# Two feed-forward layers: the activation of 14 column blocks turned by the DMA engines as two 16-bit planes, where TensorE had turned it

## The chip, the core and the metric

The kernel runs on one core of a Trainium2 chip, in float32 from end to end. The metric is the device time of one execution in microseconds (us), taken as the median of several runs. A profile is one further execution, recorded by the hardware profiler.

## What is computed

The reference is a decoder layer: a SwiGLU feed-forward layer, a mixing layer (retention and windowed attention), and a second SwiGLU layer, each on a normalised and modulated input. The change concerns the two feed-forward layers alone:

```
def swiglu(h, w_gu, w_down):
    gate, up = jnp.split(h @ w_gu, 2, axis=-1)
    return (jax.nn.silu(gate) * up) @ w_down
# S = 256 rows, D_MODEL = 2048, D_FF = 5632; called once on w_ffn1_* and once on w_ffn2_*
```

## The kernel before

A float32 product is made from halves. Each weight tile `raw` is split into a rounded part `wh` (cast on ACT, line 334) and a remainder `wl` (subtraction on DVE, line 335). The activation is held split in the same way, as `hh` and `hl` for the input of a feed-forward layer, and as pair tiles `a` for the input of the down product. Each 128x512 product then takes three matmuls: line 326 (high times high), line 327 (low times high) and line 328 (high times low).

`gemm` (lines 383 to 388) makes 512 output columns for both halves of 128 rows. It walks over K in blocks of 512 (`kb`). Each block is one DMA of 1 MB on the SP queue (`load`, line 311, four `raw` buffers) and two **half steps**. A half step is one cast, one subtraction and 12 matmuls. `wh` and `wl` have three buffers each (`wsp`), so ACT and DVE work up to three half steps ahead of TensorE.

`ffn_up` (lines 545 to 550) goes over blocks of 512 of the 5632 columns. For each it runs one gemm for the gate and one for the up half, 16 half steps in all. Then `swiglu_up` works on two tiles of 128x512, one for each half of the rows: Silu on ACT (line 537), the multiplication on DVE (line 538), and `transpose_to` (lines 412 to 417), which turns the tile on TensorE in four 128x128 pieces into a PSUM bank (line 416) and copies that to the tile `slot` that the down product reads (line 417). The first layer's blocks 0 to 5 are made in another loop at the start of the program. `ffn_up` makes blocks 6 to 10 of the first layer, and blocks 0 to 10 of the second, whose first gate half is already there when it begins.

`step()` (lines 299 to 307) is called after each K block of a gemm and advances a list of side work, `side`, by one. In the feed-forward layers this list is empty. `tick()` paces another stream beside the gemms: rows of `w_ada`, loaded on the SP queue and reduced on DVE (`ada_pass`, line 203).

Where an instruction stands on its engine is decided by the scheduler of the framework, for all engines but SP. `nc.any` leaves the choice of the engine to it as well. Each engine then runs its own list in order, and waits where it stands.

Of the kernel before, what the change touches and what calls it, by code (L numbers as in the profile page):

```python
# [8 lines left out]

F32 = mybir.dt.float32  # L10
F32R = mybir.dt.float32r
AF = mybir.ActivationFunctionType
ALU = mybir.AluOpType
AX = mybir.AxisListType
# [2 lines left out]
P = 128  # L17
S = 256
D = 2048
DFF = 5632  # L20
# [3 lines left out]
CH = 512  # L24
KB = 4
# [51 lines left out]
def layer_kernel(  # L77
# [22 lines left out]
    nc = tc.nc  # L100
# [15 lines left out]
    def nm(s):  # L116
        uid[0] += 1
        return f"{s}_{uid[0]}"
# [4 lines left out]
    def bank():  # L123
        return psm.tile([P, CH], F32, tag="ps", name=nm("ps"))

    def side_bank():
        return psd.tile([P, CH], F32, tag="pd", name=nm("pd"))

    def t512():
        return tmp.tile([P, CH], F32, tag="t512", name=nm("t"))  # L130
# [4 lines left out]
    def slot():  # L135
        return slots.tile([P, KD * S], F32, tag="slot", name=nm("slot"))

    def small(n, tag):
        return two.tile([P, n], F32, tag=tag, name=nm(tag))
# [27 lines left out]
    for j in range(D // CH):  # L167
        pt = acc_bank()
        nc.tensor.matmul(pt, ones, c_row[:, j * CH : (j + 1) * CH], start=True, stop=True)
        nc.scalar.activation(cact[:, j * CH : (j + 1) * CH], pt, AF.Silu)  # L170
    gains = one.tile([P, 3, KD], F32, tag="gains", name="gains")
# [125 lines left out]
    side = []  # L297
# [32 lines left out]
    def split(pool, tag, src, n, hi_engine="act"):  # L330
        k = src.shape[1]
        hi = pool.tile([P, 2, n], F32R, tag=tag + "h", name=nm(tag + "h"))[:, :k, :]
        lo = pool.tile([P, 2, n], F32R, tag=tag + "l", name=nm(tag + "l"))[:, :k, :]
        nc.scalar.copy(hi, src)  # L334
# [3 lines left out]
    def pair_tile():  # L338
        return asp.tile([P, 2, CH], F32, tag="a", name=nm("a"))

    class Held:


        def __init__(self):
            self.hi = one.tile([P, KD, S], F32R, tag="hh", name=nm("hh"))
            self.lo = one.tile([P, KD, S], F32R, tag="hl", name=nm("hl"))

# [3 lines left out]
    class Whole:  # L351
# [5 lines left out]
        def pair(self, k2, home=None):  # L357
# [3 lines left out]
            if home is None:  # L361
                home = pair_tile()
            hi, lo = (
                home[:, i].rearrange("p (k s) -> p k s", k=2).bitcast(F32R) for i in range(2)
            )
# [17 lines left out]
    def gemm(act, w, col0s, KT=KD):  # L383
        banks = [[acc_bank() for _ in range(NT)] for _ in col0s]
        for kb in range(KT // KB):
            gemm_part(act, w, col0s, banks, kb, KT)
            step()
        return banks

    def home_tile():  # L390

        return slots.tile([P, 2, KD * P], F32R, tag="slot", name=nm("home"))

# [18 lines left out]
    def transpose_to(dest, src_of, n, ps=None):  # L412

        ps = ps or bank()
        for j in range(n):
            nc.tensor.transpose(ps[:, j * P : (j + 1) * P], src_of(j), ident)  # L416
        nc.any.tensor_copy(dest, ps[:, : n * P])  # L417


    def rsqrt(v, n):  # L420

        r = small(n, f"rs{n}")
        q = small(n, f"rq{n}")
        nc.scalar.activation(r, v, AF.Sqrt)
        nc.vector.reciprocal(r, r)
        nc.vector.tensor_mul(q, r, r)
        nc.vector.tensor_mul(q, q, v)
        nc.vector.tensor_scalar(
            out=q, in0=q, scalar1=-0.5, scalar2=1.5, op0=ALU.mult, op1=ALU.add
        )  # L430
        nc.vector.tensor_mul(r, r, q)
        return r

    def square_sum(dest, src):
        nc.scalar.activation(side_bank(), src, AF.Square, accum_out=dest)  # L435

    def root_table():

        nc.scalar.activation(small(1, "root"), eps, AF.Sqrt)

    def inv_rms(ssq, t):
# [7 lines left out]
        )  # L449
        nc.scalar.activation(r, s, AF.Sqrt, bias=eps, scale=1.0 / D)  # L450
        nc.vector.tensor_scalar(
# [12 lines left out]
    def modulated(held, k, src, m_shift, act=False):  # L464
# [4 lines left out]
        if act:  # L469
            nc.scalar.activation(h, src, AF.Identity, bias=shift, scale=scale)  # L470
        else:
# [50 lines left out]
        square_sum(ssq[:, t * 4 + ci : t * 4 + ci + 1], xs)  # L522


    def swiglu_up(banks_g, banks_u, tiles, ci, parts=None):

        k0 = ci * KB
        dest = tiles[k0 // KD].rearrange("p (k s) -> p k s", s=S)
        kk = k0 % KD
        for t in range(NT):  # L530
            s = t512()
            g, u = banks_g[t], banks_u[t]
            if parts is not None:
                nc.vector.tensor_add(s, g, parts[0][t])
                nc.vector.tensor_add(parts[1][t], u, parts[1][t])
                g, u = s, parts[1][t]
            nc.scalar.activation(s, g, AF.Silu)
            nc.vector.tensor_mul(s, s, u)
            transpose_to(
                dest[:, kk : kk + KB, t * P : (t + 1) * P],  # L540
                lambda j: s[:, j * P : (j + 1) * P],
                KB,
            )

    def ffn_up(held, w, tiles, first, bg=None):
        for ci in range(first, DFF // CH):
            bg = bg or gemm(held, w, [ci * CH])[0]
            bu = gemm(held, w, [DFF + ci * CH])[0]
            swiglu_up(bg, bu, tiles, ci)
            bg = None  # L550

    ORDERED = {mybir.EngineType.PE, mybir.EngineType.DVE, mybir.EngineType.Activation}
# [144 lines left out]
    tiles = [slot(), part[0]]  # L697
# [102 lines left out]
    for g, ks in enumerate(groups):  # L800
        final = g == len(groups) - 1
        order = chunks if g % 2 == 0 else chunks[::-1]
        coming = iter(()) if final else group(groups[g + 1])
        due = 0 if final else 2 * len(groups[g + 1])
        stay = () if final else order[-2:]
        for i, n in enumerate(order):
            visit(n, ks, load_blocks(n, ks), n not in stay)
            last = len(order) - 2
            for _ in range((i + 1) * due // last - i * due // last if i < last else i == last):
                next(coming, None)  # L810
            if n in stay:
                continue
            if not final:
                to_parts(n)
            elif n % 2:
                swiglu_up(
                    banks.pop(n - 1), banks.pop(n), tiles, n // 2, (part_of(n - 1), part_of(n))
                )
    gate = gate_row()
    tiles.append(slot())  # L820
    place = two_rows()
    set_pace([(2, None, 0.5), (4, 1, None), (3, None, None)], 154, place, AQ)
    ffn_up(held, gu, tiles, EARLY)
    gate_load(gate, 2)
    wi = w_in[0]
# [240 lines left out]
    def gates(p):  # L1066

        sg = slot().rearrange("p (g i t n) -> p g i t n", g=2, i=2, t=NT)
        for g, off in ((0, O_GR), (1, O_GS)):
            for i in range(2):  # L1070
                b = in_chunk(off + (2 * p + i) * CH)
                for t in range(NT):
                    nc.scalar.activation(sg[:, g, i, t, :], b[t], AF.Sigmoid)
        return sg

    first = gates(0)
# [44 lines left out]
    tiles = [slot() for _ in range(3)]  # L1121
    set_pace([(8, None, 0.5)], 160, raw_row, 2)
    ffn_up(held, w_ffn2_gu[0], tiles, 0, head)
    gf = one.tile([P, KD * S], F32, tag="hh", name="gf")[:, :D]
    nc.gpsimd.dma_start(gf, norm_final[None, :].broadcast_to([P, D]))
# [82 lines left out]
```

## Time and profile before

| what | value |
|---|---|
| median of 3 runs | 2445.66 us (2443.98 to 2446.63) |
| profiled execution, its own time | 2445.11 us |
| its span, first to last instruction | 2443.3 us |
| granted TensorE clock | 0.999 |
| busy: PE, DVE, ACT | 98%, 70%, 49% of the span |
| moved by DMA | 599.08 MB |

The span is what the profile's rows add up to. The execution's own time is 1.8 us more. PE is TensorE's matmul row; matmuls overlap in it, so the time from the start of one to the start of the next says more than the length of one.

### The profile page before, as it was taken

The numbers are of one execution on the slowest core, as the hardware profiler recorded it, in microseconds if no ns is written. First come the engines' busy times: TensorE is split into PE (matmuls) and PEld (weight loads), VectorE is DVE, ScalarE is ACT, GpSimd is POOL, SyncE is SP. The second block draws the span as 40 slices with busy tenths as digits, with TensorE's granted clock in tenths as the row PEclk, the third lists the DMA queues.
The fourth block names the chain that finished last, engine by engine and source line by source line (L and its number), as shares of the span: only waits on it lengthen the run. The fifth ranks groups of instructions, "written<-read, shape, count | busy, mean of one in ns | idle before, by whom it ended". The sixth has DMA issues, their size and how long they took to land. (4 is left out here: it accounts for less than half of the span.)

```text
span 2443.3 us, 29136 instructions
## 1 busy us (share of the span) xinstructions
PE 2398.8 (98%) x10910; PEld 1957.2 (80%) x10910; DVE 1699.8 (70%) x2733; ACT 1189.8 (49%) x1614; POOL 5.7 (0%) x14
## 2 busy tenths in 40 slices
PE   7999999999999999999999999999999999999998
PEld 4778888888787777788888888887888888888886
DVE  6898877778877677886666776767655555545656
ACT  6544544444445455554544444456544444444544
POOL 0000000000000000000000000000000000000000
PEclk9999999999999999999999999999999999999999
DMA  9987688888875766666677777755666676665563
GB/s 354 338 333 273 227 310 299 333 304 299 308 264 186 243 210 219 207 217 214 239 262 252 253 254 266 266 189 172 229 227 222 224 244 220 226 225 192 186 200 121
DMA packets 244080, 599.08 MB, mean 245 GB/s; under 512 B 9633, under 2 KB 10017, under 8 KB 225121
## 3 DMA queue, kind: packets, MB, share of 16 engines
q1 hardware_dynamic: 242434, 590.56, 69.0%
q0 software_dynamic: 928, 5.61, 0.6%
q8 instruction: 85, 1.39, 0.2%
q10 hardware_dynamic: 576, 1.05, 0.1%
q14 instruction: 57, 0.47, 0.1%
HBM read 595.06 MB, written 2.12 MB: 244 GB/s over the span
## 5 line engine op out<-in xcount | busy, mean ns | idle before, releaser
L335 DVE TENSOR_TENSOR wl<-raw,wh 128x1024 fp32r<-128x1024 f32 (+1 forms) x828 | 995.7, 1207 | 592.5 <-ACT wh L334 589.5
L334 ACT CAST wh<-raw 128x1024 fp32r<-128x1024 f32 (+1 forms) x828 | 861.2, 1041 | 1031.1 <-PE pa L327 1012.1
L326 PE MATMUL pa<-wh,hh 128*128 128x512 f32 x2224 | 870.0, 392 | 3.4 <-ACT wh L334 2.9
L327 PE MATMUL pa<-wh,hl 128*128 128x512 f32 x2224 | 869.9, 391 | 2.2 <-DVE hl L476 1.8
L328 PE MATMUL pa<-wl,hh 128*128 128x512 f32 x2224 | 803.2, 393 | 4.1 <-DVE wl L335 3.9
L326 PEld LDWEIGHTS pa<-wh,hh 128*128 128x128 f32 x2224 | 417.7, 188 | 93.3 <-ACT wh L334 4.2
L328 PEld LDWEIGHTS pa<-wl,hh 128*128 128x128 f32 x2224 | 415.3, 188 | 95.5 <-DVE wl L335 10.2
L327 PEld LDWEIGHTS pa<-wh,hl 128*128 128x128 f32 x2224 | 418.0, 188 | 89.7 <-DVE hl L476 2.4
L327 PE MATMUL pa<-wh,a 128*128 128x512 f32 x992 | 383.8, 389 | 0.0
L328 PE MATMUL pa<-wl,a 128*128 128x512 f32 x992 | 367.6, 390 | 1.2 <-DVE wl L335 1.1
L326 PE MATMUL pa<-wh,a 128*128 128x512 f32 x992 | 367.2, 390 | 0.4 <-DVE t L519 0.4
L328 PEld LDWEIGHTS pa<-wl,a 128*128 128x128 f32 x992 | 185.7, 188 | 42.3 <-DVE wl L335 4.5
L326 PEld LDWEIGHTS pa<-wh,a 128*128 128x128 f32 x992 | 186.0, 188 | 40.6 <-DVE t L519 1.1
L327 PEld LDWEIGHTS pa<-wh,a 128*128 128x128 f32 x992 | 186.3, 188 | 38.5
L203 DVE CUSTOM_DVE_ANT_0 slot<-slot,cact 128x512 f32<-128x512 f32 (+1 forms) x252 | 192.8, 814 | 31.6 <-DMA slot<-in_w_ada_dram 31.3
L203 DVE CUSTOM_DVE_ANT_0 raw<-raw,cact 128x512 f32<-128x512 f32 (+1 forms) x260 | 167.0, 696 | 38.4 <-DMA raw<-in_w_ada_dram 27.8
L367 DVE TENSOR_TENSOR a<-slot,a 128x512 fp32r<-128x512 f32 x124 | 84.8, 685 | 12.9 <-ACT a L366 12.9
L366 ACT CAST a<-slot 128x512 fp32r<-128x512 f32 x124 | 76.4, 618 | 14.8 <-PE pa L328 14.7
L417 ACT COPY slot<-ps 128x512 f32<-128x512 f32 x80 | 44.7, 586 | 38.5 <-PE ps L416 38.1
L203 DVE DVE_READ_ACCUMULATOR2_ANT sums<- 128x1 f32 x512 | 42.2, 82 | 0.0
L416 PEld LDWEIGHTS ps<-small_c,t 128*128 128x128 f32 x288 | 34.4, 140 | 7.4 <-ACT slot L955 0.7
L416 PE MATMUL ps<-small_c,t 128*128 128x128 f32 x288 | 40.1, 273 | 0.0
(161 smaller groups left out, 965.7 us busy)
## 6 DMA issues: line engine op xcount, KB each, us to landing
raw<-in_w_ffn_gu_dram SPq DMA_DIRECT2D x152, 1024.0 KB, 5.2
raw<-in_w_in_dram SPq DMA_DIRECT2D x104, 1024.0 KB, 5.2
raw<-in_w_ffn_down_dram SPq DMA_DIRECT2D x88, 1024.0 KB, 5.2
slot<-in_w_ada_dram SPq DMA_DIRECT2D x76, 1024.0 KB, 7.6
raw<-in_w_ada_dram SPq DMA_DIRECT2D x64, 1024.0 KB, 4.9
raw<-in_w_ffn_gu_dram SPq DMA_DIRECT2D x24, 768.0 KB, 6.8
raw<-in_w_swa_branch_dram SPq DMA_DIRECT2D x16, 1024.0 KB, 5.3
raw<-in_w_ret_branch_dram SPq DMA_DIRECT2D x16, 1024.0 KB, 5.3
```

Of the source, the lines that this page charges most:

```text
L203: nc.vector.tensor_tensor_reduce(out=w[:, at], in0=w[:, at], in1=cact[:, at], scale=1.0, scalar=0.0, op0=ALU.mult, op1=ALU.add, accum_out= ...
L326: nc.tensor.matmul(ps, ah[:, j, ts], wh[:, j, :], start=first, stop=False)
L327: nc.tensor.matmul(ps, al[:, j, ts], wh[:, j, :], start=False, stop=False)
L328: nc.tensor.matmul(ps, ah[:, j, ts], wl[:, j, :], start=False, stop=last)
L334: nc.scalar.copy(hi, src)
L335: nc.vector.tensor_sub(lo, src, hi.bitcast(F32))
L366: nc.scalar.copy(hi, v)
L367: nc.vector.tensor_sub(lo, v, hi.bitcast(F32))
L416: nc.tensor.transpose(ps[:, j * P : (j + 1) * P], src_of(j), ident)
L417: nc.any.tensor_copy(dest, ps[:, : n * P])
```

## The change

For blocks 6 to 9 of the first layer and 0 to 9 of the second (`by_dma=ci < DFF // CH - 1`), `swiglu_up` no longer calls `transpose_to`. The tile of 128x512 float32 values is read as 16-bit words. ACT copies the low words into one plane of 128x512 and the high words into another (`apart`), and issues a transposing DMA for each plane on its own queue. Later, each turned plane is copied into its words of `slot` (`together`), on an engine that the scheduler chooses. The planes and their turned copies lie in one pair tile, of the pool that the down product uses. `later` deals this work out over the `step()` calls of the next block's gemms. Block 10 of each layer keeps the transposes on TensorE.

```
+    def words(t):
+        return t.bitcast(U16).rearrange("p (n i) -> p n i", i=2)

+    def turn_by_dma(dest, src):
+        both = pair_tile()
+        planes = both[:, 0].bitcast(U16).rearrange("p (i n) -> p i n", i=2)
+        turned = both[:, 1].bitcast(U16).rearrange("p (i k s) -> p i k s", i=2, k=KB)
+        def apart():
+            for i in range(2):
+                nc.scalar.copy(planes[:, i, :], words(src)[:, :, i])
+                nc.scalar.dma_start_transpose(turned[:, i], planes[:, i, :])
+        into = dest.bitcast(U16).rearrange("p k (s i) -> p k s i", i=2)
+        def together():
+            for i in range(2):
+                nc.any.tensor_copy(into[:, :, :, i], turned[:, i])
+        return apart, together

+    def later(work):
+        for first, _ in work:
+            yield
+            first()
+        yield
+        for _, second in work:
+            yield
+            second()
...
             nc.vector.tensor_mul(s, s, u)
+            if by_dma:
+                work.append(turn_by_dma(dest[:, kk : kk + KB, t * P : (t + 1) * P], s))
+                continue
             transpose_to(
...
+        if work:
+            side.append(later(work))
...
-            swiglu_up(bg, bu, tiles, ci)
+            swiglu_up(bg, bu, tiles, ci, by_dma=ci < DFF // CH - 1)
```

In the changed program the lines stand further down: line 334 is 335, 335 is 336, 326 to 328 are 327 to 329, and 538 is 573. The plane copies are line 432, the transposing DMAs line 433, the copies that merge the planes line 439. Counted over the program, 112 transposes of line 416 go from PE (377 of this form become 265) and 28 copies of line 417 from ACT. Added are 56 plane copies and 56 transposing DMAs on ACT, and 56 merging copies, 34 on DVE and 22 on ACT.

The next rows are those of TensorE where block 1 of the second layer ends, before. `pa` are the product banks, `t` the two tiles after the multiplication, `ps` the banks of the turned tiles, `small_c` holds the identity.

```order
L328 MATMUL pa_13883<-wl_13904,hh_12504 128x512
L326 MATMUL pa_13882<-wh_13903,hh_12504 128x512
L327 MATMUL pa_13882<-wh_13903,hl_12505 128x512
L416 MATMUL ps_13867<-small_c,t_13864 128x128 x4
L416 MATMUL ps_13876<-small_c,t_13873 128x128 x4
L328 MATMUL pa_13882<-wl_13904,hh_12504 128x512
L326 MATMUL pa_13883<-wh_13903,hh_12504 128x512
```

The eight rows of line 416 are gone in the changed program, and nothing takes their place on TensorE. ACT at the same place, before (the casts of the half steps around it, and the two copies of the turned tiles):

```order
L334 CAST wh_13921<-raw_13919 128x1024
L334 CAST wh_13937<-raw_13919 128x1024
L417 COPY slot_13413<-ps_13867 128x4x128
L417 COPY slot_13413<-ps_13876 128x4x128
L334 CAST wh_13958<-raw_13956 128x1024
L334 CAST wh_13974<-raw_13956 128x1024
```

And ACT there in the changed program; `a_13877` and `a_13881` are the pair tiles of the two halves of the rows:

```order
L335 CAST wh_13921<-raw_13919 128x1024
L432 COPY a_13877<-t_13874 128x512 x2
L432 COPY a_13881<-t_13878 128x512 x2
L433 DMA_TRANSPOSE a_13877<-a_13877 128x4x128
L335 CAST wh_13937<-raw_13919 128x1024
L433 DMA_TRANSPOSE a_13877<-a_13877 128x4x128
L433 DMA_TRANSPOSE a_13881<-a_13881 128x4x128
L335 CAST wh_13962<-raw_13960 128x1024
L433 DMA_TRANSPOSE a_13881<-a_13881 128x4x128
L335 CAST wh_13978<-raw_13960 128x1024
L439 COPY slot_13421<-a_13881 128x4x128
L335 CAST wh_14001<-raw_13999 128x1024
```

Four plane copies and four issues of a DMA now stand between three casts that followed each other, and a merging copy stands two casts later. DVE at this place, in the changed program; before, the four subtractions follow each other with nothing between them:

```order
L573 TENSOR_TENSOR t_13874<-t_13874,pa_13727 128x512
L573 TENSOR_TENSOR t_13878<-t_13878,pa_13728 128x512
L336 TENSOR_TENSOR wl_13922<-raw_13919,wh_13921 128x1024
L336 TENSOR_TENSOR wl_13938<-raw_13919,wh_13937 128x1024
L439 COPY slot_13421<-a_13877 128x4x128 x2
L439 COPY slot_13421<-a_13881 128x4x128
L336 TENSOR_TENSOR wl_13963<-raw_13960,wh_13962 128x1024
L336 TENSOR_TENSOR wl_13979<-raw_13960,wh_13978 128x1024
```

Three merging copies stand ahead of the subtraction of `wl_13963`. The third reads what the first DMA of `a_13881` wrote.

The other blocks of the second layer have this order too, leaving aside the `ada_pass` rows and, in block 9, casts for the down product, but for blocks 2, 7 and 4. In blocks 2 and 7 the merging copy on ACT stands directly behind the fourth DMA, ahead of the cast. In block 4 two DMAs stand ahead of the second cast, and two merging copies ahead of the second subtraction. In the first layer each of the four blocks has an order of its own: in block 6 one merging copy stands ahead of the second subtraction, in block 7 three ahead of the fourth, and in blocks 8 and 9 all four are on ACT, behind the fourth cast or later.

More of the change, by code (lines that the diff above doesn't have):

```diff
@@ L11 @@
 F32R = mybir.dt.float32r
+U16 = mybir.dt.uint16
 AF = mybir.ActivationFunctionType
@@ L522, in add_gated, with swiglu_up @@
         square_sum(ssq[:, t * 4 + ci : t * 4 + ci + 1], xs)
-    def swiglu_up(banks_g, banks_u, tiles, ci, parts=None):
+    def later(work):
[6 more added lines that the diff above has]
+            second()
+    def swiglu_up(banks_g, banks_u, tiles, ci, parts=None, by_dma=False):
         k0 = ci * KB
@@ L529, in swiglu_up @@
         kk = k0 % KD
+        work = []
         for t in range(NT):
```

## Prediction

> **What bounds the kernel now.** I read the page first, then the busy times by stage, then the timelines of TensorE (PE), ACT and DVE around one block of the second feed-forward layer. From the page, with three of its costliest groups:
>
> ```profile
> span 2443.3 us, 29136 instructions
> PE 2398.8 (98%) x10910; PEld 1957.2 (80%) x10910; DVE 1699.8 (70%) x2733; ACT 1189.8 (49%) x1614; POOL 5.7 (0%) x14
> ...
> L334 ACT CAST wh<-raw 128x1024 fp32r<-128x1024 f32 (+1 forms) x828 | 861.2, 1041 | 1031.1 <-PE pa L327 1012.1
> ...
> L366 ACT CAST a<-slot 128x512 fp32r<-128x512 f32 x124 | 76.4, 618 | 14.8 <-PE pa L328 14.7
> ...
> L416 PE MATMUL ps<-small_c,t 128*128 128x128 f32 x288 | 40.1, 273 | 0.0
> ```
>
> PE is busy for 98% of the span. The busy times of two stages, with DMA share and GB/s last; the first row holds the changed blocks of the first layer, the second all of the second layer's:
>
> ```profile
> 260.00:530.00 270.00, 269.92 (x1227) 223.62 (x1226) 204.03 (x354) 121.03 (x135) 1.07 (x2) 1.00 0.82 299
> 1712.00:2180.00 468.00, 467.14 (x2102) 386.85 (x2101) 262.54 (x328) 204.34 (x221) 1.06 (x2) 1.00 0.67 227
> ```
>
> There PE idles for 0.08 us of 270 and for 0.86 us of 468, at full clock. So what leaves PE's list in these stages leaves the time, and nothing more is to be had: no wait hides behind the transposes. ACT and DVE are busy for 0.44 and 0.56 of the second stage. Who waits for whom there:
>
> ```profile
> ACT wh L334 <- PE pa L327: 230.9, 143, 1.7
> DVE wl L335 <- ACT wh L334: 199.8, 144, 2.4
> ```
>
> ACT waits 1.7 us before a cast until PE gives a buffer back, and DVE waits for ACT. PE sets the pace, the other two follow it. How far ahead they are is the cover for what the change adds. One cast, its subtraction, and the matmuls that free the buffer and first use it (timelines of ACT, DVE and PE):
>
> ```profile
> 1863.52 1.05 ACT L334 CAST wh<-raw 128x1024 fp32r<-128x1024 f32 x1 [1.67 <-PE pa L327]
> 1866.24 1.05 ACT L334 CAST wh<-raw 128x1024 fp32r<-128x1024 f32 x1 [1.67 <-PE pa L327]
> ...
> 1864.61 1.23 DVE L335 TENSOR_TENSOR wl<-raw,wh 128x1024 fp32r<-128x1024 f32 x1 [1.50 <-ACT wh L334]
> ...
> 1863.10 0.39 PE L327 MATMUL pa<-wh,hl 128*128 128x512 f32 x1
> ...
> 1868.99 0.39 PE L326 MATMUL pa<-wh,hh 128*128 128x512 f32 x1
> ...
> 1869.89 0.61 PE L328 MATMUL pa<-wl,hh 128*128 128x512 f32 x2
> ```
>
> The cast starts at 1863.52, when the matmul of 1863.10 has ended. Its half step begins on PE 26 matmuls later, at 1868.99, and the remainder is first read at 1869.89. I find these two by counting in the program's order. The remainder is ready at 1864.61 + 1.23 = 1865.84. So **a half step may come up to 1869.89 - 1865.84 = 4.05 us late before PE stalls**; its subtraction must end 1869.89 - 1863.52 = 6.37 us after the time at which its cast could start. A half step lasts 1866.24 - 1863.52 = 2.72 us.
>
> **What the change removes.** Eight transposes end each block. PE there:
>
> ```profile
> 1884.17 0.39 PE L327 MATMUL pa<-wh,hl 128*128 128x512 f32 x1
> 1884.40 1.03 PE L416 MATMUL ps<-small_c,t 128*128 128x128 f32 x8
> 1885.19 0.48 PE L328 MATMUL pa<-wl,hh 128*128 128x512 f32 x1
> 1885.51 0.39 PE L326 MATMUL pa<-wh,hh 128*128 128x512 f32 x1
> ```
>
> From 1884.40 to 1885.19 PE gives 0.79 us to them, and the matmul behind them takes 0.32 us to the next start instead of 0.23, so 0.88 us in all. Over 14 blocks that is **12.4 us saved** (12.35). The two copies out of PSUM go from ACT as well, which waits there anyway: nothing.
>
> **What it adds.** No work on PE. On ACT, per block: four plane copies of 128x512 and four DMA issues. On DVE and ACT: four merging copies. By sums all this fits. ACT idles 1.67 us in each of 16 half steps, 27 us of a block. What can cost is lateness, where the added work stands in a bunch. Prices from these rows (timelines of ACT at two places and of DVE, then the DMA table):
>
> ```profile
> 1885.04 1.08 ACT L417 COPY slot<-ps 128x512 f32<-128x512 f32 x2 [1.43 <-PE ps L416]
> ...
> 2429.34 0.90 ACTq L1153 DMA_DIRECT2D out_dram<-t  x2
> ...
> 1868.47 0.69 DVE L203 CUSTOM_DVE_ANT_0 raw<-raw,cact 128x512 f32<-128x512 f32 x1
> ...
> 1879.39 1.37 DVE L538 TENSOR_TENSOR t<-t,pa 128x512 f32<-128x512 f32 x2
> ...
> raw<-in_w_ffn_gu_dram SPq DMA_DIRECT2D x152, 1024.0 KB, 5.2
> ...
> slot<-in_w_ada_dram SPq DMA_DIRECT2D x76, 1024.0 KB, 7.6
> ...
> out_dram<-t ACTq DMA_DIRECT2D x4, 256.0 KB, 3.0
> ```
>
> - A plane copy: 0.54 us, half of the pair in 1.08 (one alone took 618 ns in line 366, from SBUF as here). Four take 2.16.
> - A merging copy: 0.69 us on DVE, as an operation on 128x512 there takes, and 0.54 on ACT.
> - **c, the time for which ACT is held by issuing one transposing DMA.** No row has one. From below: a plain DMA on ACT's queue takes 0.45 us, half of 0.90. From above: the DMA fills four blocks of 128x128, and as four plain ones would take 4 x 0.45 = 1.8 us. I take the middle, 1.1 us.
> - **d, from its issue to its landing.** From below 3.0 us, a DMA of 256 KB on the same queue (these move 128 KB, but beside weight loads). From above 7.6 us, that of a 1 MB load that queues behind others. I take 5.2 us, that of the weight loads beside which these DMAs will run.
>
> [...]
>
> **The sum, for the common order of a second-layer block** (seven blocks: 0, 1, 3, 5, 6, 8, 9). Zero is when the first of the three casts, that of `wh_13921`, can start. The multiplications end 0.92 us after it (the pair that starts at 1879.39 takes 1.37; the cast beside it starts at 1879.84):
>
> ```profile
> 1879.84 1.05 ACT L334 CAST wh<-raw 128x1024 fp32r<-128x1024 f32 x1 [1.66 <-PE pa L327]
> ```
>
> So ACT goes on without a wait. The cast ends at 1.05, the four plane copies at 3.21, the first DMA is issued by 3.21 + c, the second cast ends at 4.26 + c, and the third DMA's issue starts at 4.26 + 2c. It lands at 4.26 + 2c + d. DVE stands in front of the third merging copy until then, and **behind it is queued the subtraction of `wl_13963`**, which PE needs. That ends at 4.26 + 2c + d + 0.69 + 1.23 = 6.18 + 2c + d. It must end at 2 x 2.72 + 6.37 = 11.81. PE stalls for what 2c + d is over 5.63. With c = 1.1 and d = 5.2 that is 7.4, a stall of 1.77 us; seven blocks, 12.4 us.
>
> - Blocks 2 and 7: the merging copy on ACT waits for the fourth DMA (issue at 5.31 + 3c) ahead of the fourth cast. The cast starts at 5.85 + 3c + d and may start at 8.16 + 4.05 = 12.21. Over 6.36: 8.5 - 6.36 = 2.14, twice, 4.3 us.
> - Block 4: the second DMA starts at 3.21 + c, and the subtraction behind its merge ends at 5.13 + c + d, against 9.09. Over 3.96: 2.34 us.
> - First layer, block 6: the same with the first DMA, d over 3.96: 1.24 us. Block 7: issue of the third at 5.90 + 2c, the limit 2c + d at 6.7: 0.7 us. Blocks 8 and 9 merge late on ACT, and their casts are under 4.05 us late: nothing.
>
> Stalls: 12.4 + 4.3 + 2.3 + 1.2 + 0.7 = **21.0 us** (20.9 by the rounded terms). Less 12.4 saved: **+8.6 us**. The profiled execution would go from 2445.11 us to 2453.7; the median, 0.55 us above it, from 2445.66 to 2454.3.
>
> Costed at nothing: the bytes (56 x 128 KB are 7 MB of 599); the merging copies as DVE work, hidden by the 1.50 us it waits for ACT before most subtractions, which would cost 0.69 each without that; and the waits of SP. SP's loads share completion semaphores with the new DMAs, and the program's order has loads waiting for them. But the nearest such load feeds a cast ten casts behind, 27 us, and takes 5.2 us to land.
>
> **Rivals.**
> - **No stall; the change pays** (faster). If issue and landing are those of a plain DMA, 2c + d = 3.9, under 5.63, and all of the other limits hold too: 2445.66 - 12.4 = 2433.3. For it speaks that 128 KB is an eighth of a weight load, and that the 3.0 us row is from this queue; against it, that this row comes from the program's end, where no weights are loaded. With c = 1.1 the point of balance is d = 4.5. [...]
> - **Landing as late as the slow loads.** c = 1.8 and d = 7.6: 2c + d = 11.2 and 3c + d = 13.0, stalls 7 x 5.57 + 2 x 6.64 + 3.6 + 5.4 + 4.5 = 65.8 us, so +53.4, 2499.1.
> - **The weights come late.** If a transposing DMA kept the 16 engines to itself for its 5.2 us, the first layer's 16 would take 83 us of a stage that leaves 270 x (1 - 0.82) = 49 free. The 34 us missing go to PE: about 2488. Against it: 2 MB in 80 us would be a tenth of the 299 GB/s that the same engines move there.
> - That the change does not do what it says is out: the order has the 112 transposes gone.
>
> **How the numbers follow.** A difference of 0.2%, 4.9 us, is about what a measurement of this kernel can tell from none. My forecast, a stall of one to three us a block, has 0.37, with a range of its own of 2451 to 2475. The two slower rivals have 0.20 together, no stall or stalls that sum to under 7.5 us 0.30, and the balance within 0.2% 0.13. Faster 0.30, same 0.13, slower 0.57. The range goes from the one bound to the other, 2432 to 2499.
>
> **What would show it.** PE's rows of line 416 should fall by about 112, and in stages without stalls a block should take 0.88 us less. The rows of the DMAs give d, and the time between them and the next cast gives c. If I am right, DVE's waits have line 439 waiting for the DMA, PE has new idle time put down to `wl` of line 336, and it falls on the third half step behind the multiplications, in nearly every changed block. If PE shows no such idle time, c or d was sized too large and the first rival holds. If it waits for `wh`, ACT's issuing is the cost and not the landing. If ACT waits for `raw`, the weights come late. A d under 3 us or over 8 would make the range wrong.

## The result, and the profile after

| | before | after |
|---|---|---|
| median, on the same chip | 2445.08 us (2443.91 to 2446.63) | 2456.57 us (2453.29 to 2462.14) |
| profiled execution | 2445.11 us | 2453.29 us |
| its span | 2443.3 us | 2451.4 us |
| granted TensorE clock | 0.999 | 0.996 |

The changed kernel takes 1.0048 times as long, 95% interval [1.0035, 1.0061]. The forecast was 2454.3 us (2453.7 for the profiled execution). The total was met: the profiled execution to 0.4 us, the median to 2.3. The rest of this document is about where the time came from, which is not where the forecast put it. The profiled execution is the fastest of the six, so the traces place its time, and not the 3.3 us by which the median is longer.

From the page of after, the busy times, ACT's own DMA queue (q10, 576 packets and 1.05 MB before) and the merging copies on ACT:

```profile
PE 2393.8 (98%) x10798; PEld 1950.0 (80%) x10798; DVE 1711.5 (70%) x2767; ACT 1216.2 (50%) x1664; POOL 5.6 (0%) x14
...
q10 hardware_dynamic: 31040, 8.40, 2.3%
...
L439 ACT COPY slot<-a 128x512 uint16<-128x512 uint16 x22 | 16.5, 770 | 39.2 <-DMA a<-a 39.1
```

PE has 112 instructions less (10910 before) and is busy 5 us less, yet the span is 8.1 us longer: PE waits. The queue carries 31040 - 576 = 30464 packets more, 544 for each of the 56 DMAs, that is 7.35 MB in packets of 241 bytes on average.

The same two stages as in the prediction (PE busy is the second number; PEclk, DMA share and GB/s are the last three):

```profile
260.00:530.00 270.00, 263.88 (x1173) 216.93 (x1172) 203.04 (x355) 130.78 (x155) 1.06 (x2) 0.99 0.87 299
1712.00:2180.00 468.00, 460.62 (x2018) 378.48 (x2018) 273.41 (x363) 221.08 (x257) 1.05 (x2) 0.99 0.72 235
```

PE now idles for 6.1 us in the first layer's stage (0.08 before) and for 7.4 us in the second's (0.86 before). The clock is 0.99 where it was 1.00. In the first layer's stage the DMA engines still move 299 GB/s, as before. Who waits for whom (us in total, times, longest), from the waits of PE, DVE and ACT:

```profile
PE pa L329 <- DVE wl L336: 13.8, 19, 3.7
...
PE pa L327 <- ACT wh L335: 8.0, 6, 3.2
...
DVE slot L439 <- DMA a<-a: 28.6, 13, 5.0
...
ACT slot L439 <- DMA a<-a: 39.1, 17, 4.7
...
ACT wh L335 <- issue: 14.8, 10, 2.7
```

PE's wait for `wl` was 6.9 us before and that for `wh` 2.9. Both have grown, so the lateness reaches PE by DVE and by ACT. (The waits of the last row are spread over the whole program, and 5.7 us of them, in four places, were there before.) The two rows of line 439 are the merging copies that stand and wait for a transposing DMA. They do so 30 times in 56, while PE waits only in a few places. These are all of PE's waits in the changed blocks, and the row of 662.71 in the down product (timeline of PE; the bracket is the idle time):

```profile
370.23 0.50 PE L329 MATMUL pa<-wl,hh 128*128 128x512 f32 x1 [1.33 <-DVE wl L336]
465.45 0.50 PE L327 MATMUL pa<-wh,hh 128*128 128x512 f32 x1 [3.20 <-ACT wh L335]
474.51 0.50 PE L327 MATMUL pa<-wh,hh 128*128 128x512 f32 x1 [1.49 <-ACT wh L335]
662.71 0.50 PE L327 MATMUL pa<-wh,a 128*128 128x512 f32 x1 [1.21 <-DVE t L543]
1766.95 0.50 PE L329 MATMUL pa<-wl,hh 128*128 128x512 f32 x1 [1.56 <-DVE wl L336]
1856.54 0.50 PE L327 MATMUL pa<-wh,hh 128*128 128x512 f32 x1 [0.42 <-ACT wh L335]
1946.16 0.80 PE L329 MATMUL pa<-wl,hh 128*128 128x512 f32 x1 [3.74 <-DVE wl L336]
2036.34 0.50 PE L329 MATMUL pa<-wl,hh 128*128 128x512 f32 x1 [0.47 <-DVE wl L336]
```

Seven waits in six blocks of 14: block 6 (370) and block 8 (465 and 474) of the first layer, blocks 0, 2, 4 and 6 of the second. A pause, here and below, is the time from one matmul's start to the next beyond the usual 0.23 us. It is the idle time and 0.16 us more, because a matmul's row of 0.39 us reaches past the 0.23 us after which the next one could start. The seven cost 12.2 + 7 x 0.16 = 13.3 us. The wait in the down product grew by 0.8 us.

The rest is clock. Three stretches of after, each behind such a wait:

```profile
466.50:469.90 3.40, 3.37 (x9) 2.51 (x9) 3.40 (x9) 0.06 (x1) 0.00 (x0) 0.50 1.14 302
664.50:667.80 3.30, 3.30 (x8) 2.62 (x9) 3.30 (x5) 0.00 (x0) 0.00 (x0) 0.50 0.68 249
1946.20:1951.20 5.00, 5.00 (x12) 3.94 (x13) 2.74 (x3) 1.22 (x2) 0.00 (x0) 0.50 0.55 193
```

The granted clock is 0.50 there, and PE starts a matmul every 0.43 us, where it is 0.23 at full clock. In the 11.7 us of these three stretches that loses 11.7 x (1 - 0.23 / 0.43) = 5.4 us. Before has no such stretch but at its very end. The sum: 13.3 + 0.8 + 5.4 = 19.5 us lost, 12.4 saved, +7.1 us; the two profiled executions differ by 8.2. About 1 us is not placed.

How a stall comes about, in block 0 of the second layer (timelines of ACT and DVE; ACTq is ACT's issuing):

```profile
1753.41 1.05 ACT L335 CAST wh<-raw 128x1024 fp32r<-128x1024 f32 x1 [1.67 <-PE pa L328]
1754.37 1.13 ACT L432 COPY a<-t 128x512 uint16<-128x512 uint16 x2
1755.01 1.21 ACTq L433 DMA_TRANSPOSE a<-a  x1
1755.40 1.14 ACT L432 COPY a<-t 128x512 uint16<-128x512 uint16 x2
1756.28 1.26 ACTq L433 DMA_TRANSPOSE a<-a  x1
1756.45 1.04 ACT L335 CAST wh<-raw 128x1024 fp32r<-128x1024 f32 x1
1757.63 2.27 ACTq L433 DMA_TRANSPOSE a<-a  x1
...
1765.33 0.46 DVE L439 COPY slot<-a 128x512 uint16<-128x512 uint16 x1 [4.33 <-DMA a<-a]
1765.68 2.35 DVE L336 TENSOR_TENSOR wl<-raw,wh 128x1024 fp32r<-128x1024 f32 x2
```

Read the issues of DMAs against the copies: the second pair of copies (1755.40) and the second cast (1756.45) run while a DMA is being issued. The third DMA's issue starts 4.22 us after the first cast. It lands 7.7 us later, DVE has waited 4.33 us for it, and behind it stand the subtractions that PE needs. The first of them should have ended 11.81 us after 1753.41, at 1765.22. It ends near 1766.9, 1.7 us late, and PE's row of 1766.95 shows the pause. The block of 1946.16 shows the same for its own order: the subtraction behind the second merge ended 12.95 us after the first cast, where the forecast's limit was 9.09. It was 3.86 us late, and PE paused 3.90.

All 56 issues, and the 49 landings that the trace places (ns of the issue, minimum, median and maximum; then us from issue to landing):

```profile
L433 ACTq DMA_TRANSPOSE a<-a x56: 1204/1242/4857, 358.5 to 2161.0; - x56
...
DMA to landing us min/median/max: 2.4/4.9/20.9
```

The two shortest landings, 2.42 us (issued at 2073.91) and 2.44 (at 1984.62), had a load in flight beside them for 1.0 and 1.6 us; the two longest of the second layer, 8.51 (at 1936.01) and 7.67 (at 1757.63), for 8.3 and 5.7. Of the 13 over 5 us there, 8 end within 1.3 us after a load in flight beside them has landed: in block 4 the second DMA landed 8.5 us after its issue, at 1944.52, and the load that was issued beside it at 1944.30. The 20.9 us is in block 8 of the first layer (ACT's timeline):

```profile
450.44 1.05 ACT L335 CAST wh<-raw 128x1024 fp32r<-128x1024 f32 x1 [1.57 <-issue]
...
451.82 1.05 ACT L335 CAST wh<-raw 128x1024 fp32r<-128x1024 f32 x1 [0.33 <-ACT wh L335]
451.90 4.86 ACTq L433 DMA_TRANSPOSE a<-a  x1
456.86 1.05 ACT L335 CAST wh<-raw 128x1024 fp32r<-128x1024 f32 x1 [3.98 <-PE pa L329]
...
463.74 0.76 ACT L439 COPY slot<-a 128x512 uint16<-128x512 uint16 x1 [4.73 <-DMA a<-a]
464.37 1.98 ACT L335 CAST wh<-raw 128x1024 fp32r<-128x1024 f32 x2
469.84 0.77 ACT L439 COPY slot<-a 128x512 uint16<-128x512 uint16 x1 [3.50 <-DMA a<-a]
```

The fourth issue takes 4.86 us, and the cast behind it starts as it ends. The merging copies wait for 4.73 and 3.50 us with casts queued behind them, and PE pauses at 465.45 for `wh`. What the DMA engines move in this block, ahead of the four DMAs (first row) and beside them; the last two numbers are the DMA share and GB/s:

```profile
436.00:444.00 8.00, 8.00 (x37) 6.61 (x36) 5.69 (x10) 3.09 (x3) 0.56 (x1) 1.00 1.04 416
448.00:452.00 4.00, 4.00 (x19) 3.30 (x18) 2.98 (x10) 2.10 (x4) 0.00 (x0) 1.00 1.13 215
460.00:464.00 4.00, 2.25 (x10) 1.52 (x9) 0.00 (x0) 0.27 (x1) 0.00 (x0) 1.00 1.05 130
```

By the DMA share, 1.04 to 1.13, the engines are full in all three rows, but they move 416 GB/s ahead, and 215 and 130 beside the transposing DMAs. The two loads issued just behind the first of the four land 10 and 13 us after their issue; 5.1 and 7.3 us are the medians of their kinds in this run.

### The profile page after: what moved, and what is told of

Same layout as the page of the kernel before. It is cut to its first block, busy times and chain, and to the rows that moved or that the text cites. A ratio compares the mean times of both kernels' runs of the same rounds, so it can differ in the third digit from the quotient of the medians.

```text
span 2451.4 us, 29087 instructions
## 1 busy us (share of the span) xinstructions
PE 2393.8 (98%) x10798; PEld 1950.0 (80%) x10798; DVE 1711.5 (70%) x2767; ACT 1216.2 (50%) x1664; POOL 5.6 (0%) x14
## 3 DMA queue, kind: packets, MB, share of 16 engines
q10 hardware_dynamic: 31040, 8.40, 2.3%
## 5 line engine op out<-in xcount | busy, mean ns | idle before, releaser
L368 DVE TENSOR_TENSOR a<-slot,a 128x512 fp32r<-128x512 f32 x124 | 84.8, 684 | 14.8 <-ACT a L367 14.8
L418 ACT COPY slot<-ps 128x512 f32<-128x512 f32 x52 | 29.5, 584 | 23.7 <-PE ps L417 23.5
L459 ACT ACTIVATE pd<-x_sb 128x512 f32<-128x512 f32 x32 | 19.0, 593 | 35.2 <-DVE x_sb L544 32.5
L439 ACT COPY slot<-a 128x512 uint16<-128x512 uint16 x22 | 16.5, 770 | 39.2 <-DMA a<-a 39.1
```

The costliest lines, as they stand in the source:

```text
L368: nc.vector.tensor_sub(lo, v, hi.bitcast(F32))
L439: nc.any.tensor_copy(into[:, :, :, i], turned[:, i])
```

## The experiments

Each time below is a median with its range, then its ratio to the kernel before, measured on the same chip, with the 95% interval. My theory after reading the traces: the stalls come from merging copies that stand in front of subtractions and casts before their DMA has landed, and the half clock follows from PE's pauses. The rival, as the forecast had it: ACT's issuing holds the casts (2c in the sum), or the DMAs slow the weights whatever the place of the merges.

**Late merges.** All four merging copies go to DVE, pinned behind the latest subtraction, two K blocks later:

```
         def together():
-            for i in range(2):
-                nc.any.tensor_copy(into[:, :, :, i], turned[:, i])
+            with tc.issue_after(last_sub[0].ins):
+                for i in range(2):
+                    nc.vector.tensor_copy(into[:, :, :, i], turned[:, i])
...
-        yield
+        for _ in range(3):
+            yield
```

> The four merging copies are all put on DVE and queued behind the subtractions of the next up gemm's third and fourth K block, some ten half steps later; plane copies, DMA issues and DMAs stay as they are in the changed kernel. Theory (the cost is DVE and ACT standing in front of a merging copy until its DMA has landed): the pauses of PE at wl and wh in the changed blocks go, the half-clock stretches with them, and the time is that of before less the 12.4 us of transposes, about 2433 us; issue near 1.2 us and landing near 4.9 us as now. Rival (the bunch of plane copies and issues on ACT makes the casts late): the pauses stay and the time stays above 2450 us.

Measured: 2438.22 us (2432.05 to 2440.26), 0.9963 [0.995, 0.9976] of before. Its DMAs:

```profile
L435 ACTq DMA_TRANSPOSE a<-a x56: 1204/1248/6288, 358.0 to 2143.1; - x56
...
DMA to landing us min/median/max: 2.4/4.9/20.7
```

The DMAs land as late as in after, and are issued as slowly. Yet the stalls are gone from the changed blocks, but for a pause of 1.4 us behind the issue that took 6.29 us and one of 0.35, and the clock is full until the program's very end, as before. So the loss comes from where the merges stand, and the theory holds for it. (The 22 merges that ACT had are on DVE now as well; place and engine changed together.) The 5 us that are missing to 2433 were looked for next. One thing this kernel does not take away: its loads are slower. Between 340 and 520 us, where the first layer's blocks are turned, a weight load of 1 MB lands 7.2 us after its issue at the median and 14.0 at the most, where it was 5.5 and 8.2 before.

**Plain DMAs** in place of the transposing ones, in the kernel with late merges:

```
-                nc.scalar.dma_start_transpose(turned[:, i], planes[:, i, :])
+                nc.scalar.dma_start(turned[:, i].rearrange("p k s -> p (k s)"), planes[:, i, :])
```

> As e1_late_merge, but each transposing DMA is a plain DMA of the same 128 KB on the same queue, so the planes are merged unturned and the output is not the reference's. Theory (a transposing DMA is late beside loads because it is cut into some 540 small packets, which take turns with those of the loads): issue 0.45 us, landing 2 to 3 us also beside loads. Rival (anything on ACT's queue waits behind the loads in flight): landing with a median near 4.9 us as now. The time is near that of e1_late_merge, about 2433 us, by both.

Measured: 2431.78 us (2431.27 to 2432.43), 0.9941 [0.9929, 0.9953].

```profile
L435 ACTq DMA_DIRECT2D a<-a x56: 472/566/1012, 357.3 to 2137.1; - x56
...
DMA to landing us min/median/max: 1.9/4.4/8.9
```

The median landing hardly moves, 4.4 against 4.9 us: my expectation of 2 to 3 us fell. By my reading, most of a typical landing beyond the shortest (1.9 us here) is a wait behind loads and not the turning. What the transposing form costs is the issue (0.57 against 1.25 us, at most 1.0 against 6.3), the tail (8.9 against 20.7 us) and the time of the loads beside it: a weight load between 340 and 520 us lands in 5.7 us here, at most 8.1, as before. Such a DMA is 144 packets where the transposing one is 544. The two kernels are 6.4 us apart.

**One layer alone**, the change as it was; `first == 0` is the second layer, and the other run has `first > 0` for the first:

```
-            swiglu_up(bg, bu, tiles, ci, by_dma=ci < DFF // CH - 1)
+            swiglu_up(bg, bu, tiles, ci, by_dma=ci < DFF // CH - 1 and first == 0)
```

> The change in the second layer's ten blocks alone; the first layer's four blocks transposed on TensorE as before. Theory (pauses come only where loads are in flight, as counted in the profile after: 6.8 us of pauses and 2.6 us of half clock in the second layer, against 8.8 saved): about 2446 us. Rival (the forecast's formula, 19.0 us of stalls in these ten blocks): about 2455 us.

Measured: 2441.12 us (2437.29 to 2444.34), 0.998 [0.9972, 0.9989]: a little faster than before. Both expectations, 2446 and 2455, were too high.

> The change in the first layer's four blocks alone. Theory (6.5 us of pauses there, 0.8 more in the down product and 3.4 of half clock, against 3.5 saved): about 2452 us. Rival (the forecast's formula, 1.9 us of stalls in these four blocks): about 2443 us, faster than before.

Measured: 2458.19 us (2451.67 to 2464.13), 1.0048 [1.0033, 1.0063]. The four blocks of the first layer lose as much by themselves as the whole change, and 6 us more than the theory had. The landings of the second layer alone, then of the first layer alone:

```profile
DMA to landing us min/median/max: 2.4/3.6/6.5
```

```profile
DMA to landing us min/median/max: 2.7/6.0/21.6
```

Alone, the second layer's landings end at 6.5 us, and PE pauses once in the profiled execution (2437.29 us), for 1.9 us. In the first layer an issue takes up to 5.4 us; PE pauses four times in the changed blocks, for 0.9 to 3.4 us, and the clock is 0.50 in three stretches of 3.4 us, the last of them in the down product. The rival (2443, the forecast's view that the first layer costs little) fell.

**One layer alone, with late merges.** The two conditions above, in the kernel with late merges.

> The change in the second layer alone, with the late merging copies of e1_late_merge. Theory (there the landing in front of a merging copy was the whole cost): no pause of PE at wl beyond those of before, 8.8 us saved, about 2437 us where before takes 2446. Rival (something else of the ten blocks costs as well): about 2441 us, as e3_second_only.

Measured: 2437.03 us (2435.5 to 2438.68), 0.9967 [0.9955, 0.9979], so -8.1 us where ten blocks save 8.8. The theory held for this layer.

> The change in the first layer's four blocks alone, with late merging copies. Theory (most of the 12 us that e4_first_only lost was ACT and DVE waiting for landings, and what e1_late_merge still lacked, some 4 us, lies in this layer): about 2447 us, one pause at wh in block 8, no half clock. Rival (the transposing DMAs slow the layer's weight loads whatever waits for them): near 2455 us, with ACT waiting for raw.

Measured: 2443.69 us (2441.03 to 2448.95), 0.9993 [0.9984, 1.0002]. Late merges take away the first layer's loss; its four blocks should save 3.5 us and save 1.7, with an interval from 3.9 saved to 0.5 lost. The pause at `wh` that I expected in block 8 did not come; the only one in these blocks is of 0.5 us, for `wl`.

**Late merges, block 8 of the first layer left on TensorE.**

```
-            swiglu_up(bg, bu, tiles, ci, by_dma=ci < DFF // CH - 1)
+            swiglu_up(bg, bu, tiles, ci, by_dma=ci < DFF // CH - 1 and not (first > 0 and ci == 8))
```

> As e1_late_merge, but the first layer's block 8 keeps its transposes on TensorE. Theory (what e1_late_merge still lacks comes from block 8, whose four DMAs meet two loads and the gate row's broadcast; there the fourth issue held ACT for 6.3 us): 0.9 us of saving is given up and some 3 us won, about 2435 us, no issue over 3 us. Rival (the rest is spread over the layer): 2438 us or more.

Measured: 2437.38 us (2434.7 to 2441.48), 0.9968 [0.9956, 0.9979]. This lies between the two expectations; the longest issue is 2.6 us. The profiled execution (2441.48 us) tells more. It has new pauses of 2.0 and 2.6 us for `wl` at 373 and 384 us, where block 6 is turned, and a stretch at half clock behind the second. No merging copy makes them. Ahead of each, DVE stands in front of an `ada_pass` operation, whose load is late, with subtractions queued behind it (timeline of DVE):

```profile
370.79 0.69 DVE L204 CUSTOM_DVE_ANT_0 slot<-slot,cact 128x512 f32<-128x512 f32 x1 [6.31 <-DMA slot<-in_w_ada_dram]
380.46 0.69 DVE L204 CUSTOM_DVE_ANT_0 slot<-slot,cact 128x512 f32<-128x512 f32 x1 [3.73 <-DMA slot<-in_w_ada_dram]
```

The two loads were issued beside and just behind the block's four transposing DMAs and landed after 13.5 and 17.2 us; before, the median between 340 and 520 us is 7.8 and the longest 11.1. So the rival was right in part: the DMAs slow the loads wherever the merges stand, and in this execution that reached PE. How often it does in the other executions no trace shows; it is one place where the rest of the late merges' loss can come from.

**Late merges and a spread issue.** Each plane copy and its DMA is pinned behind a cast, one in each of four K blocks:

```
-        def apart():
-            for i in range(2):
+        def apart(i):
+            with tc.issue_after(last_cast[0].ins):
                 nc.scalar.copy(planes[:, i, :], words(src)[:, :, i])
                 nc.scalar.dma_start_transpose(turned[:, i], planes[:, i, :])
```

> As e1_late_merge, but the plane copies and DMAs are pinned behind the casts of four K blocks, one plane after each, so the four DMAs of a block are issued some 5 us apart and not within 5 us. Theory (four in a bunch fill the queue; one alone does not): no issue over 2.5 us, landings in the first layer under 12 us, about 2434 us. Rival (the number of small packets costs, wherever they stand): 2438 us as e1_late_merge.

Measured: 2433.58 us (2431.1 to 2437.85), 0.9953 [0.9941, 0.9966] of before.

```profile
L435 ACTq DMA_TRANSPOSE a<-a x56: 1205/1207/1587, 357.6 to 2149.0; - x56
...
DMA to landing us min/median/max: 2.5/5.8/12.2
```

No issue takes over 1.6 us any more, and no landing over 12.2 (12 was expected). In the two stages of the prediction PE idles 0.24 and 0.53 us; the only wait of PE in a changed block is the one of 0.24 us. The loads are still slower than before (a weight load lands in 6.8 us between 340 and 520 us, at most 12.0), but here PE waits for none of them. Of the versions that turn the planes it is the fastest, 12 us ahead of before and 23 ahead of after.

**Pauses with nothing of the change.** Was the half clock the work of the pauses, or of the new DMA traffic? In the kernel before, one cast is written over several times in blocks 1, 3, 5, 7 and 9 of the second layer, so that ACT alone comes late:

```
-        nc.scalar.copy(hi, src)
+        for _ in range(1 + again.pop("now", 0)):
+            nc.scalar.copy(hi, src)
...
+        more = {1: 5, 3: 6, 5: 7, 7: 8, 9: 10} if first == 0 else {}
```

> The kernel before, with nothing of the change in it. In blocks 1, 3, 5, 7 and 9 of the second layer one cast is written 6, 7, 8, 9 and 11 times over, which only makes ACT late: at 1.05 us a cast and 4.05 us of cover TensorE should pause for about 1.2, 2.3, 3.3, 4.4 and 6.5 us there, 17.6 us in all. My theory is that the half clock in the changed kernel follows a pause of over some 3 us, whatever makes it: then TensorE's granted clock is 0.5 for 3 to 7 us after the last two or three of these pauses, the two short ones leave it full, and the time goes up by 17.6 + 5 to 8 us, to about 2469. The rival is that the half clock has another cause in the changed kernel (the transposing DMAs, or the DMA traffic): then the clock stays full behind all five pauses and the time is about 2463.

Measured: 2484.57 us (2480.46 to 2485.64), 1.0159 [1.0142, 1.0176]. The five pauses (timeline of PE), and the us behind the first and the second (PEclk is third from the end):

```profile
1786.38 0.50 PE L326 MATMUL pa<-wh,hh 128*128 128x512 f32 x1 [2.93 <-ACT wh L337]
1879.91 0.50 PE L326 MATMUL pa<-wh,hh 128*128 128x512 f32 x1 [4.01 <-ACT wh L337]
1975.93 0.80 PE L326 MATMUL pa<-wh,hh 128*128 128x512 f32 x1 [5.08 <-ACT wh L337]
2073.01 0.79 PE L326 MATMUL pa<-wh,hh 128*128 128x512 f32 x1 [6.16 <-ACT wh L337]
2173.17 0.79 PE L326 MATMUL pa<-wh,hh 128*128 128x512 f32 x1 [8.31 <-ACT wh L337]
```

```profile
1786.40:1791.40 5.00, 4.94 (x20) 3.77 (x21) 4.20 (x4) 1.05 (x1) 0.00 (x0) 1.00 0.34 87
1880.80:1884.20 3.40, 3.40 (x9) 2.45 (x8) 2.58 (x3) 0.00 (x0) 0.00 (x0) 0.50 0.47 146
```

Each pause is about two casts longer than I had worked out, because the scheduler put two later casts between the repeats. The five come to 26.5 us idle + 5 x 0.16 = 27.3 us, where 17.6 were expected. The question is settled all the same: without any transposing DMA, the shortest pause leaves the clock full and the four longer ones halve it, for 17.6 us behind them in all. The rival fell. At the rate of above these 17.6 us cost 8.2. The kernel is 40.3 us slower. Of the 4.8 us left, some 3 were already lost when the second layer began, ahead of the edited blocks.

## Why the prediction was right, and where it was not

- **PE is the bound, and 12.4 us leave it**: right. With the merges and the issue out of the way the change gives 2433.58 us, beside the 2433.3 of the forecast's first rival.
- **The cover, and what is queued behind the third merging copy**: right, to 0.1 us in the three blocks of the second layer where DVE stood there too long. Blocks 0, 4 and 6 missed the forecast's due times by 1.7, 3.9 and 0.6 us, and PE paused 1.72, 3.90 and 0.63.
- **The prices of the copies**: four plane copies 2.17 us in block 0 (2.16 taken), a merge 0.46 on DVE (0.69) and 0.77 on ACT (0.54). No consequence.
- **c, "the time for which ACT is held by issuing"**: this step failed in what it stood for, not in its size. An issue takes 1.24 us (1.1 taken). But ACT copies and casts meanwhile, so most of it adds nothing: the third DMA left at 4.22 us (4.2 to 4.5 in all ten blocks of the second layer) and not at 4.26 + 2 x 1.1 = 6.46. The condition for a block of the common order was thus 4.22 + d + 0.46 for the merge + 1.23 for the subtraction under 11.81, that is d under 5.9 us, and not 2c + d under 5.63. It sorts the seven blocks: d of the third DMA was 7.7 and some 6.4 us in the two that stalled, 2.4 to 4.8 in the other five. Only where issues pile up does one hold a cast: of the 14.8 us that casts waited for an issue, 6.6 lie in the changed blocks, in four places; in block 8 the issue of 4.86 us comes on top.
- **d = 5.2 us**: the median is 4.9, but d is no constant. It goes from 2.4 to 20.9 us with the loads in flight. With the looser condition the typical block of the second layer has no stall, and only a few have one: not 1.77 us in seven blocks, 2.14 in two and 2.34 in one, 19.0 together, but four pauses in ten blocks, of 0.6 to 3.9 us, 6.8 together.
- **Block 6 of the first layer**: 1.24 us were forecast, 1.49 found, by luck. The first DMA, on which the forecast put it, landed after 3.2 us, and its merge held up nothing. The pause came from the second merging copy, ahead of the third subtraction, which the sum left out: it stood for 4.98 us until 368.62. Block 7, with 0.7 us forecast, had no pause.
- **"Blocks 8 and 9 merge late on ACT, and their casts are under 4.05 us late: nothing"**: wrong for block 8, the costliest place of all. Two pauses of 3.4 and 1.7 us and a stretch at half clock come from d of 11 to 21 us and an issue of 4.9. The forecast gave the first layer 1.9 us in all; changed alone, it makes the kernel 1.0048 times as long, as the whole change does.
- **The clock**: neither in the sum nor among what was costed at nothing. It is 5.4 of the 19.5 us.
- **The total**: 21.0 us of stalls were forecast, 19.5 found and about 1 not placed, in the profiled execution; by the medians it is 23.9 (11.5 longer, 12.4 saved). That it met is luck, for two errors offset each other: many small stalls in the second layer that did not come, against long ones in the first and a clock that were left out.
- **The rivals**: "no stall" is what the kernel with late merges and a spread issue shows. "Landing as late as the slow loads" did happen, and worse, but in one block. "The weights come late" did not hold for the stage (299 GB/s as before), though single loads did come late: in block 8, up to 15.6 us after their issue, and in the run without block 8, where PE paused for it. Its price of 2488 was short by its own working: the second layer's 40 DMAs would take 208 us of a stage that leaves 468 x (1 - 0.67) = 154 free, and these 54 us were not counted.
- **"What would show it"**: the waits of line 439 and the idle time on `wl` came; "nearly every changed block" did not, and the waits for `wh` showed the part on ACT.

Open: what holds an issue for 4.7 to 6.3 us. An issue that long occurs once in each of four runs, in the first layer, with four issues in a row beside loads, and it is gone when they are spread or plain; no run isolates the cause. Open too: how much of what the late merges still lack comes from late loads. Nor is it settled why the second layer's landings are shorter when that layer is changed alone (median 3.6 us, at most 6.5, and the same with late merges).

## What to carry to other kernels

Moving work off the bound engine pays only if nothing that waits for the new path stands in front of what the bound engine needs: here the change took 1.0048 times as long as before with the merging copies ahead of subtractions and casts, and 0.9963 times with them behind, on DVE. Place the consumer of a DMA late in its engine's order, by the tail of the landings (20.9 us here) and not the median (4.9). Take the landing time of a small DMA from the loads it will share the engines with, place by place, and ask what those loads will be late for in turn. Count a pause of TensorE twice where it halves the clock, as one of 3.20 us did here and one of 1.56 did not: for its length, and for the clock behind it (in after 13.3 us of pauses in the changed blocks and 5.4 of clock).

## What the runs showed of the hardware

- **The clock falls by windows.** In each run with several of them, the stretches at half clock begin on a grid of 3.413 us (in the run with made pauses at 1880.80, 1972.96, 2071.95 and 2167.52, which are 27, 29 and 28 such steps apart; in after at 466.47, 664.45 and 1944.44, 58 and 375 apart). I counted PE's busy share in each such window, 0.23 us for every matmul started. Over the eleven profiles (before, after and the nine experiments), between 200 and 2400 us, each window that led from full into half clock had 37% or less, and no window from 42% up did. That is why a wait of 1.21 us in the down product, with a short one of 0.40 behind it, halves the clock at 664 in after, and 2.93 us at 1786, which falls across two windows (43% and 53%), doesn't in the run with made pauses. The same two waits of the down product, at 656 in the run with late merges, left the clock full: there the emptier window had 57%. Not all of the windows that led into half clock were empty: the one ahead of 1944.44 in after had 36%.
- **ACT works while its queue issues**: copies and casts that were ready ran inside issues of 1.2 us (in after the copies of 1755.40 in the issue of 1755.01, the cast of 1756.45 in that of 1756.28); a cast that stands behind the issue waits for its end (the cast of 450.44, after 1.57 us of idling).
- **Transposing DMAs slow the loads beside them.** A weight load between 340 and 520 us lands in 7.2 us at the median with them and in 5.7 with plain ones, in the same kernel; at the most in 14.0 and 8.1. At a DMA share of 1.05 to 1.13, 130 to 215 GB/s moved beside four in a row in block 8; ahead of them it was 416 at 1.04. It is not so at every moment: with the DMAs spread, 379 to 388 GB/s moved while their packets did (456 to 468 us). A transposing DMA is 544 packets and a plain one 144; that this is the reason is not shown.
